# Gated blocks exchanged from SBUF to SBUF, and down's left-side sums begun a group earlier, in a hybrid decoder block on Trainium2

## The chip, the cores and the metric

The kernel runs on one core of one Trainium2 chip. A core has five engines: TensorE (PE; its weight loads are shown apart, as PEld), VectorE (DVE), ScalarE (ACT), GpSimd (POOL) and SyncE (SP). Each has its own queue of instructions and works through it in order; they meet at semaphores. SP, ACT and POOL can issue DMA transfers, and all transfers of the core share 16 DMA engines. SBUF and PSUM are the memories on the chip, each with 128 partitions.

The metric is the device time in microseconds (us) of one execution. The median of three runs before the change is 1948.04 us (1947.73 to 1949.59).

## The reference, cut to what matters

256 rows of 2048 numbers go through one decoder block, all in float32:

```
h = h + 0.5 * swiglu(rms_norm(h, ffn1_norm), ffn1_w_gu, ffn1_w_down)
h = h + hybrid_mixer(rms_norm(h, mix_norm), ...)
h = h + 0.5 * swiglu(rms_norm(h, ffn2_norm), ffn2_w_gu, ffn2_w_down)
gate = sigmoid(rms_norm(h, ple_norm) @ ple_w_gate)
h = h + gate * (p @ ple_w_proj)
out = rms_norm(h, final_norm)

def swiglu(x, w_gu, w_down):
    gate, up = split(x @ w_gu, 2)
    return (silu(gate) * up) @ w_down
```

The change lies in the two swiglu blocks: 2048 inputs, 5632 gate and 5632 up columns, and 2048 outputs each.

## The kernel before, in words

**Products in two halves.** Each float32 operand is split into a high part, rounded to the matmul's type, and a low part, the rest. A product is then three matmuls: high by high, high by low, low by high. For weights a **pair** is a load of 512 KB by SP (line 74, buffers raw, four of them), a cast by ACT (whi, line 77) and a subtraction by DVE (wlo, line 78); it serves 12 matmuls of 128 x 512. `next_weights` (line 85) asks for pairs up to two ahead of their use.

**Groups.** A swiglu block works on 11 column blocks of 512 in three **parts** of 3, 4 and 4 blocks (line 27). For each block a gate/up group ("gu") multiplies the normed input by the gate's block (banks g0, g1 for the two halves of 128 rows) and the up block (u0, u1). When a part's blocks are there, two "dn" groups multiply them by the part's rows of w_down, and add the result to h. At the second swiglu's end one more group ("behind") starts the next gate's product.

**Seven products for eight.** In most groups the first steps of the contraction are done by a seven-product scheme (`SEVEN`, `product`, line 327; tiles shi and slo, lines 298 and 299, are the high and low halves of sums of weights R). It needs sums of the left operand too: `halves` (line 423) makes them on DVE as S, by one addition of the halves (line 455) and four sums (line 461), and splits S into Sh (ACT, line 463) and Sl (DVE, line 464). There is one Sh and one Sl. Four of the seven products read them. The seven products of a group run one by one between the plain pairs of the group in front of it, its *follower* in the code. For down a part with 4 blocks has three steps in the scheme, so its S is made in two pieces; a part with 3 blocks has two, one piece.

**The gated block.** At a gu group's end, silu(gate) comes from ACT (tile sil, line 508) and DVE multiplies it by up (line 480). The block must then be transposed for down: DVE transposes within 32 x 32 tiles (tile tb, line 485), four DMA writes bring quarters of the partitions to DRAM (line 491), and one DMA reads all of it back in the other order (tile tT, line 496). ACT and DVE split it into hTh and hTl (lines 502 and 503), down's left operand.

**What sets the order.** Python generators in `Lanes` (line 720) are advanced one step after each plain pair (`lanes.step`, line 546), and so place side work between pairs. Lane 0 holds the exchange of a gated block, lane 1 the sums. From the traced program a scheduler makes each engine's final order: an instruction that is ready may move ahead, unless `keep_in_program_order` ties it behind its predecessor. Tiles of one tag share their buffers, and a later tile waits until the earlier one's readers are done. In the swiglu's pool the tags sil and tT have one buffer each; S, sil and tb, tT are spread over them.

Of the kernel before, what the change touches and what calls it, by code (L numbers as in the profile page):

```python
# [20 lines left out]
NB = 512  # L21
# [9 lines left out]
NS_DOWN = tuple(3 if i1 - i0 == 4 else 2 for i0, i1 in PARTS)  # L31


SEVEN = (0, 1, 2, 4, 3, 5, 6)
# [12 lines left out]
def block_kernel(ctx, tc, a, out):  # L47
    nc = tc.nc
# [4 lines left out]
    act = ctx.enter_context(tc.tile_pool(name="act", bufs=1))  # L53
# [9 lines left out]
    lanes = Lanes(4)  # L63
    dr = ctx.enter_context(tc.tile_pool(name="dr", bufs=1, space=bass.MemoryType.DRAM))
# [358 lines left out]
    def halves(kind, his, los, ns, wait=0):  # L423


        for _ in range(wait):
            yield
        fp = current[0]

        sh = fp.tile([P, NS, 2, 2, P], F32R, tag="Sh", name="Sh")  # L430
        sl = fp.tile([P, NS, 2, 2, P], F32R, tag="Sl", name="Sl")

        def side(i, g):
            if i in (0, 4, 6):
                k, t = 2 * (g % 2) + (i > 0), i // 6
                c = slice(t * P, (t + 1) * P)
                return his[g // 2][:, k, c], los[g // 2][:, k, c]
            j, t = {1: (1, 1), 2: (0, 0), 3: (0, 1), 5: (1, 0)}[i]
            return sh[:, g, j, t, :], sl[:, g, j, t, :]

        sides[kind] = side

        for g0 in range(0, ns, 2):
            n = min(2, ns - g0)
            hi, lo = his[g0 // 2], los[g0 // 2]
            keep = lambda ins: ins
            if g0 and n == 1:

                keep = tc.keep_in_program_order
                yield  # L450
            if n == 2:
                x = fp.tile([P, 2 * NB], F32, tag="sil", name="S")
            else:
                x = act.tile([P, NB], F32, tag="nat", name="S", bufs=4)
            keep(nc.vector.tensor_tensor(out=x, in0=hi[:, 0:2 * n].bitcast(F32).rearrange("p k x -> p (k x)"),
                                         in1=lo[:, 0:2 * n].bitcast(F32).rearrange("p k x -> p (k x)"), op=ALU.add))
            xv = x.rearrange("p (g j t y) -> p g j t y", g=n, j=2, t=2)
            a11, a12, a21, a22 = (xv[:, :, j, t, :] for t in range(2) for j in range(2))
            for o, y, z, op in ((a22, a21, a22, ALU.subtract), (a21, a11, a21, ALU.subtract),
                                (a11, a22, a11, ALU.subtract), (a12, a11, a12, ALU.add)):  # L460
                nc.vector.tensor_tensor(out=o, in0=y, in1=z, op=op)
            sx = [y[:, g0:g0 + n].rearrange("p g j t y -> p (g j t y)") for y in (sh, sl)]
            nc.scalar.copy(sx[0], x)
            nc.vector.tensor_tensor(out=sx[1], in0=x, in1=sx[0], op=ALU.subtract)
            yield

    def ffn(n, nT, r, scale, next_norm, stat):
        xs = picker(*nT)
        late = callable(r)
        with tc.tile_pool(name="ffn", bufs=1) as fp:  # L470
            hTh, hTl = [], []

            def down_input(u, sil, th, tl, last):

                queue, keep = (nc.sync, lambda x: x) if last else (nc.scalar, tc.keep_in_program_order)
                for t in range(2):
                    nc.vector.scalar_tensor_tensor(out=sil[:, t, :], in0=u[t], scalar=r[:, t:t + 1], in1=sil[:, t, :],  # L480
                                                   op0=ALU.mult, op1=ALU.mult)
                yield
                tb = fp.tile([P, 4, 2, P], F32, tag="tT", name="tb")
                for t in range(2):
                    nc.vector.transpose(tb[:, :, t].rearrange("p c (j x) -> p c j x", j=4),
                                        sil[:, t, :].rearrange("p (j c x) -> p c j x", j=4, c=4))
                if not last:
                    yield
                scr = dr.tile([P, 4, 2, P], F32, tag="scr2", name="scr2", bufs=2)
                for q in range(4):  # L490
                    keep(queue.dma_start(out=scr[:, q].rearrange("(c x) t i -> x c (t i)", c=4),
                                         in_=tb[32 * q:32 * q + 32].rearrange("x c t i -> x c (t i)")))
                for _ in range(2 if last else 4):
                    yield
                tT = fp.tile([P, 4, 2, P], F32, tag="tT", name="tT")
                keep(nc.sync.dma_start(out=tT, in_=scr))
                for _ in range(last or 6):
                    yield
                for t in range(2):
                    hi, lo = (x[:, :, t * P:(t + 1) * P].rearrange("p j (q y) -> p q j y", q=4) for x in (th, tl))  # L500
                    tv = tT[:, :, t].rearrange("p q (j y) -> p q j y", j=4)
                    keep(nc.scalar.copy(hi, tv))  # L502
# [8 lines left out]
            nxt = None  # L511
            current[0] = fp
            lanes.add(1, halves("gu", *nT, NS, 6 if late else 0))
            for group, todo in ffn_plan[n]:
                if group.kind == "behind":
                    break
                dn = group.kind == "dn"
                i0 = PARTS[group.part][0]

                if dn and group.nb and not group.last:  # L520
                    lanes.add(1, halves("gu", *nT, NS))
                elif dn and group.nb and group.follower:
                    lanes.add(1, halves("behind", *nxt, NS_BEHIND, 4))
                elif not dn and group.follower.kind == "dn":
                    lanes.add(1, halves("dn", hTh[i0:], hTl[i0:], NS_DOWN[group.part]))
                if dn and group.last and nxt is None:
                    nxt = new_nT()
                if group.banks is None:
                    group.new_banks()
                for kind, one in todo:  # L530
                    if kind == "seventh":
                        group.follower.product(SEVEN[one])
                        continue
                    b, g = one
                    whi, wlo = next_weights()
                    for j in range(2):
# [3 lines left out]
                        for t in range(2):  # L540
# [3 lines left out]
                            nc.tensor.matmul(out, xh[:, c], wlo[:, j, :], start=False, stop=False, skip_group_check=True)  # L544
                            nc.tensor.matmul(out, xl[:, c], whi[:, j, :], start=False, stop=sp, skip_group_check=True)  # L545
                    lanes.step()
                    if g < len(group.src[b]) - 1:
                        continue
                    outs = group.banks[2 * b:2 * b + 2]
                    if dn:  # L550
                        nb = group.nb + b
                        for t in range(2):
                            hb = h[:, t, block(nb)]
                            nc.vector.scalar_tensor_tensor(out=hb, in0=outs[t], scalar=scale, in1=hb,
                                                           op0=ALU.mult, op1=ALU.add)
                            if group.last:
                                sumsq(stat, t, block(nb), nb)
                        if group.last:
                            norm_block(nxt, next_norm, nb, lambda: fp.tile([P, 2, 4, P], F32, tag="tT", name="tT"),
                                       mm_ps if group.follower or n == "2" else mx_ps)  # L560
                            lanes.advance(0)
                    elif b == 0:
                        if not late:
                            sil = gated(outs)
                    else:
                        if late:
                            r = r()
                            sil = gated(group.banks[0:2])
                            late = False
# [12 lines left out]
                        if last:  # L582
                            lanes.advance(0)
# [797 lines left out]
```

## Time and profile before

| | |
|---|---|
| median of the runs | 1948.04 us |
| the profiled execution | 1948.68 us, span 1947.0 us |
| TensorE busy | 1930.5 us, 99% of the span, 8884 matmuls |
| DVE, ACT, POOL busy | 81%, 60%, 8% |
| mean granted TensorE clock | 0.999 of full speed |
| moved by DMA | 475.04 MB, 244 GB/s |

The profile is of one execution. Its page gives each engine's busy time; views of the trace give groups of instructions by line, the waits (who waited for whom, total us, times, longest), the chain of work that ended last, and timelines with a row for each instruction or run of like ones: start, length, engine, line, operation, out<-in. "SPq" and "ACTq" are these engines' issues of DMAs. Matmuls overlap, so that a row's length is more than the distance to the next start.

### The profile page before, as it was taken

The numbers are of one execution on the slowest core, as the hardware profiler recorded it, in microseconds if no ns is written. First come the engines' busy times: TensorE is split into PE (matmuls) and PEld (weight loads), VectorE is DVE, ScalarE is ACT, GpSimd is POOL, SyncE is SP. The second block draws the span as 40 slices with busy tenths as digits, with TensorE's granted clock in tenths as the row PEclk, the third lists the DMA queues.
The fourth block names the chain that finished last, engine by engine and source line by source line (L and its number), as shares of the span: only waits on it lengthen the run. The fifth ranks groups of instructions, "written<-read, shape, count | busy, mean of one in ns | idle before, by whom it ended". The sixth has DMA issues, their size and how long they took to land.

```text
span 1947.0 us, 24130 instructions
## 1 busy us (share of the span) xinstructions
PE 1930.5 (99%) x8884; PEld 1593.0 (82%) x8884; DVE 1569.3 (81%) x1679; ACT 1163.5 (60%) x1358; POOL 148.4 (8%) x226
## 2 busy tenths in 40 slices
PE   9999999999999999999999999999999999999998
PEld 8888888888888888878788888888888888888886
DVE  7889878997889766797856579899888987888865
ACT  7656666566565557664555456566565755656654
POOL 0011100000010000010100000010000100001000
PEclk9999999999999999999999999999999999999999
DMA  8778888788887765556565786788898987888764
GB/s 314 267 238 282 254 296 273 229 294 250 279 284 240 225 219 170 176 171 208 171 204 160 242 290 227 225 291 283 243 281 249 314 260 240 272 255 293 232 213 144
DMA packets 144182, 475.04 MB, mean 244 GB/s; under 512 B 19649, under 2 KB 47297, under 8 KB 129857
## 3 DMA queue, kind: packets, MB, share of 16 engines
q1 hardware_dynamic: 107200, 302.16, 43.9%
q0 software_dynamic: 25920, 160.44, 30.2%
q10 hardware_dynamic: 10944, 10.91, 1.8%
q8 instruction: 69, 1.13, 0.2%
q14 instruction: 49, 0.39, 0.1%
HBM read 451.44 MB, written 22.02 MB: 243 GB/s over the span
## 4 chain that ended last, share of the span: by engine, by line
PE 88%; DVE 7%; DMA 3%; ACT 1%; issue 1%; POOL 0%; SPq 0%; POOLq 0%; DVEq 0%; ACTq 0%
PE d L545 5%; PE d L543 5%; PE d L544 5%; PE g L343 4%; PE g L344 4%; PE g L342 4%; PE u L544 4%; PE u L545 4%; PE u L543 4%; PE g L544 4%; PE g L545 4%; PE pj L112 4%; PE pj L113 4%; PE pj L114 4%; PE g L543 4%; PE d L343 2%
## 5 line engine op out<-in xcount | busy, mean ns | idle before, releaser
L77 ACT CAST whi<-raw 128x1024 fp32r<-128x1024 f32 (+1 forms) x489 | 512.1, 1050 | 422.7 <-PE pj L114 99.0
L78 DVE TENSOR_TENSOR wlo<-raw,whi 128x1024 fp32r<-128x1024 f32 (+1 forms) x489 | 592.3, 1218 | 162.3 <-ACT whi L77 161.2
L299 DVE TENSOR_TENSOR slo<-R,shi 128x2048 fp32r<-128x2048 f32 (+2 forms) x224 | 444.9, 1989 | 140.0 <-ACT shi L298 138.2
L298 ACT CAST shi<-R 128x2048 fp32r<-128x2048 f32 (+2 forms) x224 | 373.5, 1671 | 128.5 <-DVE R L307 62.7
L112 PE MATMUL pj<-whi,nTh 128*128 128x512 f32 x448 | 179.4, 401 | 0.0
L113 PE MATMUL pj<-wlo,nTh 128*128 128x512 f32 x448 | 175.2, 391 | 1.1 <-DVE wlo L78 1.1
L114 PE MATMUL pj<-whi,nTl 128*128 128x512 f32 x448 | 174.9, 390 | 0.0
L543 PE MATMUL d<-whi,hTh 128*128 128x512 f32 x448 | 174.5, 390 | 0.0
L544 PE MATMUL d<-wlo,hTh 128*128 128x512 f32 x448 | 174.3, 389 | 0.0
L545 PE MATMUL d<-whi,hTl 128*128 128x512 f32 x448 | 173.4, 389 | 0.0
L544 PE MATMUL g<-wlo,nTh 128*128 128x512 f32 x400 | 156.0, 390 | 0.5 <-DVE wlo L78 0.5
L544 PE MATMUL u<-wlo,nTh 128*128 128x512 f32 x400 | 155.7, 389 | 0.4 <-DVE wlo L78 0.4
L545 PE MATMUL g<-whi,nTl 128*128 128x512 f32 x400 | 155.8, 389 | 0.0
L545 PE MATMUL u<-whi,nTl 128*128 128x512 f32 x400 | 155.7, 389 | 0.0
L543 PE MATMUL g<-whi,nTh 128*128 128x512 f32 x400 | 155.3, 390 | 0.0
L543 PE MATMUL u<-whi,nTh 128*128 128x512 f32 x400 | 154.1, 389 | 0.0
L307 DVE TENSOR_TENSOR R<-R 128x2048 f32<-128x2048 f32 (+2 forms) x68 | 135.8, 1996 | 0.1
L113 PEld LDWEIGHTS pj<-wlo,nTh 128*128 128x128 f32 x448 | 84.2, 188 | 18.9 <-DVE wlo L78 2.6
L543 PEld LDWEIGHTS d<-whi,hTh 128*128 128x128 f32 x448 | 84.1, 188 | 18.2 <-ACT hTh L502 1.0
L545 PEld LDWEIGHTS d<-whi,hTl 128*128 128x128 f32 x448 | 84.1, 188 | 17.8
L114 PEld LDWEIGHTS pj<-whi,nTl 128*128 128x128 f32 x448 | 84.1, 188 | 17.5
L544 PEld LDWEIGHTS d<-wlo,hTh 128*128 128x128 f32 x448 | 84.1, 188 | 17.4
(332 smaller groups left out, 3444.1 us busy)
## 6 DMA issues: line engine op xcount, KB each, us to landing
raw<-in_w_gu SPq DMA_DIRECT2D x199, 512.0 KB, 5.7
raw<-in_w_down SPq DMA_DIRECT2D x112, 512.0 KB, 6.9
raw<-in_w_in SPq DMA_DIRECT2D x112, 512.0 KB, 3.4
R<-in_w_gu2q POOLq DMA_DIRECT2D x54, 1024.0 KB, 8.6
R<-in_w_gu1q POOLq DMA_DIRECT2D x48, 1024.0 KB, 8.6
raw<-in_w_out SPq DMA_DIRECT2D x32, 512.0 KB, 4.5
tT<-scr SPq DMA_DIRECT2D x22, 512.0 KB, 5.0
R<-in_w_down11q POOLq DMA_DIRECT2D x12, 768.0 KB, 6.2
```

The source lines that it names most:

```text
L77: nc.scalar.copy(hi[:, j, :], raw[:, j, :])
L78: nc.vector.tensor_tensor(out=lo[:, j, :], in0=raw[:, j, :], in1=hi[:, j, :], op=ALU.subtract)
L112: nc.tensor.matmul(outs[t], xh[:, c], whi[:, j, :], start=st, stop=False)
L113: nc.tensor.matmul(outs[t], xh[:, c], wlo[:, j, :], start=False, stop=False)
L114: nc.tensor.matmul(outs[t], xl[:, c], whi[:, j, :], start=False, stop=sp)
L298: keep(nc.scalar.copy(hi, w))
L299: nc.vector.tensor_tensor(out=lo, in0=w, in1=hi, op=ALU.subtract)
L307: keep(nc.vector.tensor_tensor(out=self.raw[x], in0=self.raw[x], in1=self.raw[y], op=ALU.add))
L343: nc.tensor.matmul(out, xh, wlo[:, g, :], start=False, stop=False, skip_group_check=True)
L543: nc.tensor.matmul(out, xh[:, c], whi[:, j, :], start=st, stop=False, skip_group_check=True)
L544: nc.tensor.matmul(out, xh[:, c], wlo[:, j, :], start=False, stop=False, skip_group_check=True)
L545: nc.tensor.matmul(out, xl[:, c], whi[:, j, :], start=False, stop=sp, skip_group_check=True)
```

## The change

Four things are edited, all in `halves` and `ffn`.

- The exchange: sixteen transfers, all issued by SP, go straight from tb to tT in SBUF, each 32 partitions by 1 KB: quarter q of tb's partitions, column group c, goes to quarter c of tT's partitions, group q. The DRAM scratch, its four writes and the read are gone. ACT issues no transfers here any more.
- Tags: tT takes the buffer of sil, and S takes the buffer of tb (tag tT), for pieces of both lengths. The second piece of S is no longer tied to program order and has no empty step ahead of it.
- Steps: the transfers come four steps after the product with up, the casts two steps later. In a part's last block the transfers come at once and the casts at the step they had. For a group in the seven-product scheme, silu(gate) is taken two pairs after the gate's last pair instead of right behind it.
- Down's sums are traced behind the sixth of the seven products of a part's last gu group (these run in the group in front of it), with their first piece right there; before, they were added at the start of that last group.

```diff
-            keep = lambda ins: ins
-            if g0 and n == 1:
-                keep = tc.keep_in_program_order
-                yield
-            if n == 2:
-                x = fp.tile([P, 2 * NB], F32, tag="sil", name="S")
-            else:
-                x = act.tile([P, NB], F32, tag="nat", name="S", bufs=4)
+            x = fp.tile([P, 2 * NB], F32, tag="tT", name="S")[:, 0:n * NB]
...
-                queue, keep = (nc.sync, lambda x: x) if last else (nc.scalar, tc.keep_in_program_order)
+                keep = (lambda x: x) if last else tc.keep_in_program_order
...
-                if not last:
+                for _ in range(0 if last else 3):
                     yield
-                scr = dr.tile([P, 4, 2, P], F32, tag="scr2", name="scr2", bufs=2)
+                tT = fp.tile([P, 4, 2, P], F32, tag="sil", name="tT")
                 for q in range(4):
-                    keep(queue.dma_start(out=scr[:, q].rearrange("(c x) t i -> x c (t i)", c=4),
-                                         in_=tb[32 * q:32 * q + 32].rearrange("x c t i -> x c (t i)")))
-                for _ in range(2 if last else 4):
-                    yield
-                tT = fp.tile([P, 4, 2, P], F32, tag="tT", name="tT")
-                keep(nc.sync.dma_start(out=tT, in_=scr))
-                for _ in range(last or 6):
+                    for c in range(4):
+                        keep(nc.sync.dma_start(out=tT[32 * c:32 * c + 32, q], in_=tb[32 * q:32 * q + 32, c]))
+                for _ in range(last or 2):
                     yield
...
-                elif not dn and group.follower.kind == "dn":
-                    lanes.add(1, halves("dn", hTh[i0:], hTl[i0:], NS_DOWN[group.part]))
...
                     if kind == "seventh":
-                        group.follower.product(SEVEN[one])
+                        follower = group.follower
+                        follower.product(SEVEN[one])
+                        if not dn and one == 5 and follower.kind == "gu" and follower.follower.kind == "dn":
+                            lanes.finish(1)
+                            lanes.add(1, halves("dn", hTh[i0:], hTl[i0:], NS_DOWN[group.part]))
+                            lanes.advance(1)
                         continue
...
+                    if waiting:
+                        waiting -= 1
+                        if not waiting:
+                            sil = gated(group.banks[0:2])
...
                     elif b == 0:
-                        if not late:
+                        if group.ns:
+                            waiting = 2
+                        elif not late:
                             sil = gated(outs)
...
-                        last = (3 if i1 - i0 == 4 else 2) if len(hTh) == i1 else 0
+                        last = (5 if i1 - i0 == 4 else 4) if len(hTh) == i1 else 0
```

More of the change, by code (lines that the diff above doesn't have):

```diff
@@ L445, in halves @@
             hi, lo = his[g0 // 2], los[g0 // 2]
-            keep = lambda ins: ins
-            if g0 and n == 1:
-                keep = tc.keep_in_program_order
-                yield
-            if n == 2:
-                x = fp.tile([P, 2 * NB], F32, tag="sil", name="S")
-            else:
-                x = act.tile([P, NB], F32, tag="nat", name="S", bufs=4)
-            keep(nc.vector.tensor_tensor(out=x, in0=hi[:, 0:2 * n].bitcast(F32).rearrange("p k x -> p (k x)"),
-                                         in1=lo[:, 0:2 * n].bitcast(F32).rearrange("p k x -> p (k x)"), op=ALU.add))
+            x = fp.tile([P, 2 * NB], F32, tag="tT", name="S")[:, 0:n * NB]
+            nc.vector.tensor_tensor(out=x, in0=hi[:, 0:2 * n].bitcast(F32).rearrange("p k x -> p (k x)"),
+                                    in1=lo[:, 0:2 * n].bitcast(F32).rearrange("p k x -> p (k x)"), op=ALU.add)
             xv = x.rearrange("p (g j t y) -> p g j t y", g=n, j=2, t=2)
@@ L509, in gated @@
                 return sil
-            nxt = None
+            nxt, waiting = None, 0
             current[0] = fp
```

## The prediction, on record before the result

> **What bounds the kernel now.** I read the page's first part, then the waits of TensorE's weight loads, then TensorE's own timeline where these waits lie.
>
> ```profile
> span 1947.0 us, 24130 instructions
> PE 1930.5 (99%) x8884; PEld 1593.0 (82%) x8884; DVE 1569.3 (81%) x1679; ACT 1163.5 (60%) x1358; POOL 148.4 (8%) x226
> PEld d L343 <- DVE slo L299: 4.8, 8, 0.6
> PEld d L543 <- ACT hTh L502: 1.0, 4, 0.3
> ```
>
> TensorE is busy for 99% of the span, and the change takes no matmul away. So only stalls between matmuls can be won. The longest kind within the feed-forward blocks is a down product (tile d, line 343) that waits for the low half of a weight sum (slo), eight times. Two of the eight, in TensorE's timeline, and the last of all, in the chain of waits:
>
> ```profile
> 368.20 0.40 PE L545 MATMUL u<-whi,nTl 128*128 128x512 f32 x1
> 368.73 0.50 PE L343 MATMUL d<-slo,hTh 128*128 128x512 f32 x1
> 369.07 0.40 PE L344 MATMUL d<-shi,hTl 128*128 128x512 f32 x1
> ...
> 376.34 0.39 PE L344 MATMUL d<-shi,Sl 128*128 128x512 f32 x1
> 376.57 0.39 PE L342 MATMUL d<-shi,hTh 128*128 128x512 f32 x1
> 377.18 0.50 PE L343 MATMUL d<-slo,hTh 128*128 128x512 f32 x1 [0.22 <-DVE slo L299]
> 377.52 0.40 PE L344 MATMUL d<-shi,hTl 128*128 128x512 f32 x1
> ```
> ```profile
> 1769.44 0.50 PE d L343
> ```
>
> The first number of a row is its start. A matmul normally starts 0.23 us after the one before (376.34 to 376.57). Here the distances are 0.53 and 0.34, then 0.61 and 0.34: an excess of 0.30 + 0.11 + 0.38 + 0.11 = **0.90 us** for a pair of waits. Eight waits are four pairs, one at the end of part 1 and of part 2 in either feed-forward block: 4 x 0.90 = **3.6 us**. Why slo is late there, by the timeline of DVE with the group of line 461, and by that of ACT:
>
> ```profile
> 345.68 1.22 DVE L455 TENSOR_TENSOR S<-hTh,hTl 128x1024 f32<-128x1024 f32 x1
> L461 DVE TENSOR_TENSOR S<-S 128x256 f32<-128x256 f32 (+1 forms) x92 | 36.7, 399 | 0.9
> 354.09 0.69 DVE L455 TENSOR_TENSOR S<-hTh,hTl 128x512 f32<-128x512 f32 x1
> 363.59 0.68 DVE L464 TENSOR_TENSOR Sl<-S,Sh 128x512 fp32r<-128x512 f32 x1
> 366.92 1.76 DVE L299 TENSOR_TENSOR slo<-R,shi 128x1536 fp32r<-128x1536 f32 x1 [2.65 <-ACT shi L298]
> ```
> ```profile
> 364.92 0.57 ACT L347 COPY d<-d 128x512 f32<-128x512 f32 x1 [1.99 <-PE d L344]
> 365.40 1.48 ACT L298 CAST shi<-R 128x1536 fp32r<-128x1536 f32 x1
> ```
>
> Down's left-side sums S take from 345.68 to 364.27, in two pieces between other work of DVE. Only then can the products that use Sh and Sl end. ACT sits 1.99 us until TensorE is through, copies (364.92), makes the next shi (365.40), DVE makes slo of it (366.92 to 368.68), and TensorE, which has no other matmul left that is ready, starts at 368.73. The late end of S is the cause.
>
> **The change, step by step.** Durations are those of the profiled execution, 1948.68 us (1.7 more than its span). The median of the runs is 1948.04, 0.64 lower; the sum is moved by that at its end.
>
> *1. Down's sums earlier.* They are now written behind the sixth product of the last gate/up group, where the last reader of the old Sh stands, and no longer after the first pair of that group. That is three turns of 12 matmuls ahead (a pair, a product, a pair: 36 x 0.23 = 8 us), and the second piece's empty step and forced order go as well. No operation is added. DVE's share of S is 1.22 + 0.69 + 8 x 0.40, and for the two Sl 1.23 (the first piece's form, as at 1828.53 below) + 0.68: 7.0 us. Is there room in front? Two stretches, the group in front and the last group; the number in the third place behind the length is DVE's busy time:
>
> ```profile
> 297.40:338.00 40.60, 40.60 (x180) 33.62 (x180) 34.66 (x26) 25.01 (x24) 3.96 (x6) 1.00 0.87 265
> 338.00:368.70 30.70, 30.60 (x134) 24.60 (x133) 26.29 (x32) 16.40 (x19) 1.77 (x2) 1.00 0.77 227
> ```
>
> If all of S moved, the front would hold 41.7 of 40.6 us and the last group 19.3 of 30.7. The 1.1 us too much spill over the border, where DVE then has 11 us free. So S ends before the last group's second down product, the products follow their plan, and the four places lose **-3.6 us**. Bounds: 0 (the stall moves) and -4.6 (the waits for hTh, at most 1.0 in all, go too). I take -3.6, since the rows show the cause from end to end.
>
> *2. The exchange.* Removed in each of 22 gated blocks: four writes of 128 KB to DRAM and one load of 512 KB. In 16 blocks ACT issued the writes, in the last block of the six parts SP did. Added: sixteen SP transfers of 32 KB from SBUF to SBUF, with no wait between them and no second trip. The groups of transfers (KB, then us from issue to landing) and SP's timeline at a part's last block:
>
> ```profile
> sc<-dec SPq DMA_DIRECT2D x8, 32.0 KB, 2.4
> raw<-in_w_down SPq DMA_DIRECT2D x112, 512.0 KB, 6.9
> ```
> ```profile
> 381.90 1.78 SPq L491 DMA_DIRECT2D scr<-tb  x4
> 384.71 1.45 SPq L74 DMA_DIRECT2D raw<-in_w_down  x2
> ```
>
> The trace holds no transfer from SBUF to SBUF. Four writes of the same partitions and row length keep SP for 1.78 us, 0.45 each; sixteen take 7.1 us, and by the 32 KB row the last lands 2.4 later: 9.5 us. Today it is 13.1 us from 381.90 to the cast of hTh at 395.03 (next fence). Bounds: 16 x 0.63 + 6.9 = 17 us, were each as slow to issue as the slowest row below and the landing that of a weight load, and 9.5. I take 9.5, from the rows nearest in size and shape. Data that come sooner are worth 0, for hTh ends none of the eight waits; ACT's issue time goes too, and as no matmul waits for that I count nothing.
>
> [...]
>
> *3. What stands behind the sixteen on SP.* SP also loads the split weights, and a load behind the burst is late by up to 7.1 us. In a part's last block, by the timelines of ACT, DVE and PE:
>
> ```profile
> 393.12 1.04 ACT L77 CAST whi<-raw 128x1024 fp32r<-128x1024 f32 x1
> 395.03 1.14 ACT L502 CAST hTh<-tT 128x512 fp32r<-128x512 f32 x2 [0.87 <-DMA tT<-scr]
> 396.55 0.59 ACT L350 COPY part<-d 128x512 f32<-128x512 f32 x1 [0.38 <-PE d L344]
> 397.03 1.48 ACT L298 CAST shi<-R 128x1536 fp32r<-128x1536 f32 x1
> 398.55 1.76 DVE L299 TENSOR_TENSOR slo<-R,shi 128x1536 fp32r<-128x1536 f32 x1
> 402.02 0.39 PE L343 MATMUL d<-slo,Sh 128*128 128x512 f32 x1
> ```
>
> The burst runs from 381.90 to 389.0. The load issued at 384.71 leaves 4.3 us later, lands (6.9) at 395.9, and its cast of 393.12 is 2.8 late. Behind that cast in ACT's queue stand hTh, a copy, shi, and through shi DVE's slo. ACT now idles 0.87 + 0.38 = 1.25 us there, which takes up part of it: slo is 1.55 late. It ends at 400.31 and is used at 402.02, a cover of 1.71, so TensorE waits 0. Without ACT's idle time it would be 1.1 us, at the four last blocks of this kind (parts 1 and 2) 4.4. I take 0. The first block of all is tighter (DVE, PE and the chain of waits):
>
> ```profile
> 54.20 0.70 DVE L485 STREAM_TRANSPOSE tb<-sil 128x512 f32<-128x512 f32 x1
> 64.86 3.49 DVE L78 TENSOR_TENSOR wlo<-raw,whi 128x1024 fp32r<-128x1024 f32 x3
> 71.48 0.39 PE L544 MATMUL g<-wlo,nTh 128*128 128x512 f32 x1
> 57.01 7.52 DMA raw<-in_w_gu
> ```
>
> The load of 57.01 lands at 64.53 and is split at once, as the third of the wlo that end at 68.35, for the matmul at 71.48: cover 3.1. A burst from 54.9 to 62.0 holds it 5.0 us, so TensorE waits **+1.9**, once. Between 0 (the load goes first) and 1.9 I take 1.9, since the transfers are ready 2 us before that load. In the other blocks a pair comes only every second turn and its load has twice that time: 0.
>
> *4. Shared tiles and Silu.* S now shares a buffer with tb, and tT with sil. Silu moves two pairs later and waits for the block before to have left the buffer (hTl, DVE); behind it in ACT's queue stand the casts of weights. hTl is written in the step before, and the product that reads Silu follows two pairs later: 0, up to the cover of 1.71 us if DVE is late by more. At the end of the second feed-forward block, S of the group behind shares its buffer with the norms' tT. S is written one step ahead of the second norm's tT, so it goes first: 0.
>
> Sum: 1948.68 - 3.6 + 1.9 = 1947.0, less 0.64 = **1946.3 us** as the median, 0.09% less. A measurement of this kernel can tell about 0.2% (3.9 us) from no change.
>
> **The other ways.**
>
> *Nothing is added:* the tight load goes ahead of the transfers, and all of step 1's bound is won: 1948.04 - 4.6 = 1943.4, faster. For it: ACT, freed of 64 issues, and the shorter exchange can only help there. Against: it needs every one of these stalls, and the waits for hTh are ended by ACT's order as much as by data.
>
> *The stall moves:* DVE, over-full in front, gives S or the slo of the last gate/up products late, and TensorE waits there instead: 1948.0. Against it: 11 us free in the last group.
>
> *SP holds the weights (slower):* an issue takes more than 0.45 us.
>
> ```profile
> 1821.01 2.54 SPq L186 DMA_DIRECT2D tT<-scr  x4
> ```
>
> Four issues of another pattern take 0.63 each. At that rate the burst is 10.2 us, the load of 384.71 leaves 7.4 late, its cast is 5.9 late, and past idle time and cover 2.9 remain, at four places 11.6. The first block pays 8.1 - 3.1 = 5.0. With step 1's gain: 1948.04 - 3.6 + 16.6 = 1961.0. By the same sum the last blocks begin to pay at a burst of 7.3 us, the gain is used up at 7.6 (0.47 an issue), and the kernel is 0.2% slower at 8.4 (0.52). [...] Against: the row nearest in shape, and the scheduler may put a load between two transfers.
>
> *The group behind waits:* if the second norm had the shared buffer first, S would start after its split, not before.
>
> ```profile
> 1820.62 1.23 DVE L455 TENSOR_TENSOR S<-nTh,nTl 128x1024 f32<-128x1024 f32 x1
> 1828.53 1.23 DVE L464 TENSOR_TENSOR Sl<-S,Sh 128x1024 fp32r<-128x1024 f32 x1 [0.73 <-ACT Sh L463]
> 1833.76 1.67 DVE L162 SCALAR_TENSOR_TENSOR nTl<-tT,gains,nTh 128x256 fp32r<-128x256 f32 x4
> L544 PE MATMUL d<-wlo,hTh 128*128 128x512 f32 x16 | 6.2, 389 | 0.0
> ```
>
> The sums take 9.1 us from 1820.62 to 1829.76. Begun at 1835.4 they end at 1844.6, and the plain matmuls that were left after 1829.9 (16 of each of three kinds, 48 x 0.23 = 11.0 us) last to 1840.9: 3.7 us of wait, 1950.0. Against it: the order of writing.
>
> **Chances.** The forecast 0.42 (own range 1944.2 to 1948.5), nothing added 0.20, the stall moves 0.11, SP holds 0.22, the group behind 0.05. Faster by over 0.2% is below 1944.1: the second case and a little of the first, 0.23. Slower is above 1951.9: the SP case and a little of the last, 0.24. The same: 0.53. The range, 1943.2 to 1955.0, holds the first three cases, the last, and the SP case while its burst is only a little long; about 0.15 is left above and 0.05 below.
>
> **What would show it.** Right: no wait of d L343 for slo at the four places; S ended before the last group's second down product; sixteen issues within some 7 us; hTh's cast within 13 us of the transposes. Wrong: ACT's whi waiting for raw loads by microseconds, or matmuls waiting for wlo or slo right behind the bursts, for then step 3 was too low. If the four stalls stay though S is early, the cause in step 1 is wrong.

## The result

The changed kernel takes **2010.25 us** (median of 4 runs, 2008.99 to 2013.38) against 1948.72 us before (1947.73 to 1949.59): a ratio of 1.0318, 95% interval 1.0300 to 1.0336. It is 3.2% slower. The forecast was 1946.3 us, with a range up to 1955.0; the direction belongs to the rival "SP holds the weights", whose own price was 1961.

### The profile after

First the page of the changed kernel, its own execution of 2008.99 us: span, engines, and the chain that ended last by engine and by line.

```profile
span 2007.3 us, 24510 instructions
PE 1949.3 (97%) x8884; PEld 1600.4 (80%) x8884; DVE 1571.1 (78%) x1679; ACT 1163.5 (58%) x1358; POOL 148.5 (7%) x226
PE 63%; DVE 12%; DMA 10%; SPq 6%; issue 5%; ACT 3%; POOL 0%; DVEq 0%; ACTq 0%; POOLq 0%
```

The work is the same: 8884 matmuls, and DVE and ACT busy within 2 us of before. The span is 60.3 us longer. SP's queue (SPq) now stands in the chain that sets the end, with 6% of the span. TensorE's longest waits, two of ACT's, and these two of ACT's before the change:

```profile
PE d L343 <- DVE slo L299: 16.5, 13, 1.7
PE g L343 <- DVE slo L299: 10.6, 5, 4.1
PE d L342 <- ACT shi L298: 9.5, 6, 2.1
```
```profile
ACT whi L77 <- DMA raw<-in_w_gu: 56.6, 18, 6.5
ACT hTh L490 <- DMA tT<-tb: 40.5, 8, 8.3
```
```profile
ACT hTh L502 <- DMA tT<-scr: 4.5, 4, 1.4
ACT whi L77 <- DMA raw<-in_w_gu: 3.2, 8, 0.7
```

The columns are total us, number of waits and the longest. ACT's rows show two ways in which the transfers cost: weight loads (raw) that leave late, and the exchanged input (tT) that lands late. There is a third: S now shares tb's buffer, so it cannot be written before the transfers have read tb. In five places DVE waited 21.0 us for that. A sixth goes under another name, as one block shows. SP and DVE, by their timelines:

```profile
314.17 14.08 SPq L484 DMA_DIRECT2D tT<-tb  x16
328.35 11.23 SPq L74 DMA_DIRECT2D raw<-in_w_gu  x5
```
```profile
316.23 2.36 DVE L78 TENSOR_TENSOR wlo<-raw,whi 128x1024 fp32r<-128x1024 f32 x2
...
320.70 1.23 DVE L78 TENSOR_TENSOR wlo<-raw,whi 128x1024 fp32r<-128x1024 f32 x1
...
324.90 1.22 DVE L78 TENSOR_TENSOR wlo<-raw,whi 128x1024 fp32r<-128x1024 f32 x1
```

The sixteen issues take SP from 314.17 to 328.25. In that time DVE makes four wlo, and each of them frees one of the four raw buffers, at 317.5, 318.6, 321.9 and 326.1. All four stand empty until SP gets to the loads at 328.35. So the first load is held for 10.9 us, and ACT stands idle for it until 334.61. But TensorE's stop here does not come from that load. ACT, DVE and TensorE, by their timelines:

```profile
326.18 1.91 ACT L298 CAST shi<-R 128x2048 fp32r<-128x2048 f32 x1
334.61 1.04 ACT L77 CAST whi<-raw 128x1024 fp32r<-128x1024 f32 x1 [6.52 <-DMA raw<-in_w_gu]
```
```profile
333.73 1.23 DVE L447 TENSOR_TENSOR S<-hTh,hTl 128x1024 f32<-128x1024 f32 x1 [7.61 <-DMA raw<-in_w_gu]
...
335.81 2.29 DVE L299 TENSOR_TENSOR slo<-R,shi 128x2048 fp32r<-128x2048 f32 x1
```
```profile
338.15 0.56 PE L343 MATMUL g<-slo,Sh 128*128 128x512 f32 x1 [4.10 <-DVE slo L299]
```

TensorE waits for slo. Its input shi was ready at 328.09, but S stood in front of slo in DVE's order, and DVE was idle for 7.61 us before S. The row puts that wait down to a weight load. S reads no weights, though, and the load it names, issued at 328.35, is first used by ACT at 334.61, after S has begun. What S must wait for are the readers of tb: the last of the sixteen transfers, issued at 327.66, took 5.8 us to land, at 333.4, and S starts at 333.73. So this stop comes from the shared buffer behind a long burst. What the held load alone would have cost here, the trace does not tell.

```profile
333.60:338.10 4.50, 0.45 (x2) 0.03 (x1) 4.37 (x5) 3.49 (x4) 0.00 (x0) 1.00 0.78 320
338.10:342.00 3.90, 3.85 (x10) 3.06 (x11) 3.90 (x5) 1.93 (x4) 0.55 (x1) 0.56 0.59 188
```

These are two stretches of the same place: TensorE's busy time and matmuls, then the other engines; the number behind POOL's is the granted clock of TensorE. TensorE stands for 4.3 us, and when it goes on, matmuls start 0.43 us apart and not 0.23 (338.50, 338.93, 339.36 and so on to 341.49), at a granted clock of 0.56: ten matmuls in 3.9 us, where 17 fit.

Over all 22 bursts, by the same reading, the first load behind a burst leaves 7.6 to 14.2 us after its buffer was free, 9.8 on average. A burst is 10.0 to 14.8 us long, 11.9 on average. The row of line 484 says why (ns, least, median, most):

```profile
L484 SPq DMA_DIRECT2D tT<-tb x352: 507/590/2041, 55.3 to 1837.9; - x176
```

With the 0.05 us between two issues, the median pitch is 0.64 us, where the prediction took 0.45. On top of it 59 of the 352 issues took over 0.7 us. In front of each burst SP also stood until tb was made, 78.9 us in 22 waits.

Where TensorE's time went can be counted. Outside the mixer, take the excess: what the distance between the starts of neighbouring matmuls has beyond 0.227 us. Excesses over 0.3 us, the stops, hold 6.1 us before and 53.1 after; those between 0.1 and 0.3 hold 3.0 and 16.6. The two differences, 47.0 + 13.6 = 60.6 us, are the longer span. Of the small ones, 55 after and none before are the step of 0.40 to 0.46 us of the slow clock; they hold 11.0 us, so nearly a fifth of the loss is the slow clock behind the stops and not the stops.

Each stop can also be followed back, from the matmul to what it waited for and on along the engines, until a transfer ends the wait (with S put down to the transfers that it waits for, as above). Of the 53.1 us, about 16 go back to hTh waiting for tT, about 14 to S waiting for tb's readers, and about 19 to casts of weights waiting for their loads; under 5 us end elsewhere. So the late input, by its two ways, stopped TensorE for longer than the held loads did.

The slow clock came behind some stops and not behind others. Behind the stop above (4.3 us) the granted clock was 0.50 from 338.46 to 341.87, for 3.4 us, with the matmuls 0.43 us apart. It was 0.50 for 3.4 us as well behind two stops of 1.9 and 2.0 us that lie 2.3 us apart (407.99 and 410.24) and behind a single one of 2.7 us (596.81). It was not behind single stops of 1.6 us (389.23 and 1564.34), nor behind one of 3.0 us (1513.76). No run shows what decides it.

### The profile page after: what moved, and what is told of

It reads as the page before. It is cut to its first block, busy times and chain, and to the rows that moved or that the text cites. A ratio compares the mean times of both kernels' runs of the same rounds, so it can differ in the third digit from the quotient of the medians.

```text
span 2007.3 us, 24510 instructions
## 1 busy us (share of the span) xinstructions
PE 1949.3 (97%) x8884; PEld 1600.4 (80%) x8884; DVE 1571.1 (78%) x1679; ACT 1163.5 (58%) x1358; POOL 148.5 (7%) x226
## 4 chain that ended last, share of the span: by engine, by line
PE 63%; DVE 12%; DMA 10%; SPq 6%; issue 5%; ACT 3%; POOL 0%; DVEq 0%; ACTq 0%; POOLq 0%
SPq L484 6%; DMA raw<-in_w_gu 5%; PE pj L112 4%; PE pj L113 4%; PE pj L114 4%; PE d L535 3%; PE d L536 3%; PE d L534 3%; DVE slo L299 3%; DVE wlo L78 3%; PE g L343 3%; PE g L344 3%; PE g L342 3%; PE g L535 3%; PE g L536 3%
## 5 line engine op out<-in xcount | busy, mean ns | idle before, releaser
L299 DVE TENSOR_TENSOR slo<-R,shi 128x2048 fp32r<-128x2048 f32 (+2 forms) x224 | 444.8, 1986 | 99.6 <-ACT shi L298 98.1
L114 PEld LDWEIGHTS pj<-whi,nTl 128*128 128x128 f32 x448 | 84.1, 188 | 17.6
```

What stands on the lines that cost most here:

```text
L114: nc.tensor.matmul(outs[t], xl[:, c], whi[:, j, :], start=False, stop=sp)
L299: nc.vector.tensor_tensor(out=lo, in0=w, in1=hi, op=ALU.subtract)
```

## The experiments

Theory Q: the burst holds SP's queue, and weight loads stand behind it. Against it theory L: the exchanged input lands too late, or waits on shared buffers. Theory T: the traffic of the small packets. Theory S: the earlier sums do it. All times are medians, against the kernel before on the same chip. For two kernels "lost by" a point is the difference of the start times of the n-th matmul, of 8884 in either.

### The exchange without the earlier sums, and the sums without the exchange

```diff
 (e1: changed kernel)
-                        if not dn and one == 5 and follower.kind == "gu" and follower.follower.kind == "dn":
-                            lanes.finish(1)
-                            lanes.add(1, halves("dn", hTh[i0:], hTl[i0:], NS_DOWN[group.part]))
-                            lanes.advance(1)
+                elif not dn and group.follower.kind == "dn":
+                    lanes.add(1, halves("dn", hTh[i0:], hTl[i0:], NS_DOWN[group.part]))
```

> The changed kernel with down's left-side sums put back to where they stood before (behind the first pair of a part's last group); the sixteen transfers, the buffers and the later silu stay. Theory Q (the burst holds SP's queue, and weight loads stand behind it): the loss stays, 2005 to 2020 us, and the bursts are as long as in the changed kernel (10 to 15 us each). Theory S (the earlier sums make the loss, because they share a buffer with the transposed block and wait for its transfers): most of the loss goes, under 1970 us.

Measured: **2027.5 us**, ratio 1.0408 (1.0392 to 1.0424). This is above theory Q's range. The exchange is the loss, and the earlier sums took 17 us off it. They had to: S now shares a buffer with the transposed block tb, and so does not start before the transfers have read the tb in front of it. What ended DVE's idle time before S, in this run:

```profile
DMA tT<-tb: 31.3, 7
```

Theory S falls as it was put: the earlier sums are not the loss, they escape part of it. The shared buffer is another matter: followed back as above, about 33 us of this run's 65 us of stops end at S waiting for the transfers.

```diff
 (e2: kernel before; parts 1 and 2)
-        for g0 in range(0, ns, 2):
-            n = min(2, ns - g0)
+        one = kind == "dn"
+        for g0 in range(0, ns, 1 if one else 2):
+            n = 1 if one else 2
...
+            if one:
+                x = act.tile([P, NB], F32, tag="nat", name="S", bufs=4)
...
+                        if group.part and not dn and one == 5 and follower.kind == "gu" and follower.follower.kind == "dn":
+                            lanes.finish(1)
+                            lanes.add(1, halves("dn", hTh[i0:], hTl[i0:], NS_DOWN[group.part]))
+                            lanes.advance(1)
```

> The kernel before with only down's sums earlier, in parts 1 and 2: the first two quarters behind the sixth product of the group in front, one quarter at a time in a buffer of the activations' pool (so no buffer is shared with a transfer); the third quarter in the first step of the last group, since its input comes through DRAM only then. Step 1 of the prediction taken alone: the four waits of 0.9 us at the ends of parts 1 and 2 shrink or go, 1944 to 1948 us against 1948.7. If the stall only moves, or DVE is over-full in front, 1948 to 1950.

Measured: **1953.78 us**, ratio 1.0024 (1.0015 to 1.0033), a little slower, and above both ranges. TensorE's waits of d L343 for slo shrink only from 4.8 us (8 times) to 3.7 (5 times), and in front of each of the four places, 9 to 14 us ahead, there is a new stop of 1.4 us, one of them here:

```profile
353.26 0.61 PE L548 MATMUL u<-whi,nTh 128*128 128x512 f32 x2
355.11 0.50 PE L549 MATMUL u<-wlo,nTh 128*128 128x512 f32 x1 [1.23 <-DVE wlo L78]
```
```profile
334.00:356.00 22.00, 20.77 (x92) 16.90 (x91) 20.88 (x33) 8.92 (x11) 1.43 (x2) 1.00 0.62 171
```

DVE is busy for 20.88 of those 22 us, and wlo is late. That is the rival "the stall moves", in this form of the edit: it sums a quarter at a time, in more and shorter instructions, and the third quarter has to wait for an input that still comes at the old step. So it does not yet judge the earlier sums as the change makes them; the last run does.

### Transfers that nobody waits for

```diff
 (e3: kernel before)
+                idle = act.tile([P, NB], F32, tag="junk", name="idle", bufs=1)
+                for q in range(4):
+                    for c in range(4):
+                        keep(nc.sync.dma_start(out=idle[32 * c:32 * c + 32, 128 * q:128 * q + 128],
+                                               in_=tb[32 * q:32 * q + 32, c, 0]))
```

> The kernel before, with sixteen more transfers of SP in each gated block, from the transposed block into a scratch buffer that nobody reads (512 bytes a row, half the bytes of the real ones), just ahead of the load of the transposed block. Theory Q: nobody waits for them, and it loses all the same, as SP issues 16 x 0.64 us ahead of the weight loads: 1985 to 2015 us. Theory L (the loss is that the exchanged block itself lands late, or that it shares buffers): 1948 to 1955 us.

Measured: **2075.69 us**, ratio 1.0652 (1.0635 to 1.0668). Sixteen more issues in a block cost here even where no data depend on them. But the run lost more than expected, and not cleanly: the kernel's own load of tT stands behind the sixteen, so its input is late as well, and SP also waited for the scratch buffer:

```profile
SPq L501 <- DMA idle<-tb: 28.1, 19, 4.9
```
```profile
PE d L548 <- ACT hTh L507: 40.1, 6, 10.7
```

So it does not rule theory L out.

### Four at a time

```diff
 (e4: changed kernel)
-                for _ in range(0 if last else 3):
-                    yield
                 tT = fp.tile([P, 4, 2, P], F32, tag="sil", name="tT")
                 for q in range(4):
                     for c in range(4):
                         keep(nc.sync.dma_start(out=tT[32 * c:32 * c + 32, q], in_=tb[32 * q:32 * q + 32, c]))
-                for _ in range(last or 2):
+                    yield
+                for _ in range(last - 4 if last else 1):
                     yield
```

> The changed kernel with the sixteen transfers handed out four at a time over four steps of the lanes, so that one or two weight loads stand between; the input is cast in the same step as before. Theory Q: a hold of 4 x 0.64 = 2.6 us is inside the loads' cover, most of the loss goes: 1950 to 1975 us. Theory L or a theory of traffic (the small packets slow the weight transfers): as many transfers and bytes, and the last of them later, so no better than 2010 us.

Measured: **2014.76 us**, ratio 1.0338 (1.0323 to 1.0352): no better, which is theory L's or T's number and not Q's. But the edit did not do what it says, as SP's timeline shows:

```profile
313.17 0.33 SPq L74 DMA_DIRECT2D raw<-in_w_gu  x1
316.59 14.27 SPq L482 DMA_DIRECT2D tT<-tb  x16
330.95 11.32 SPq L74 DMA_DIRECT2D raw<-in_w_gu  x5
```

Only the first block's were apart. In the other 21 the sixteen still go out side by side, though weight loads are written between the fours: the order on the queue is the scheduler's, and it had put them together. The run tells nothing on length; a later one does it by data.

### Another queue

```diff
 (e5: changed kernel; e6: the same for q of 2 and 3 alone; e7: e5 with e1's edit)
-                        keep(nc.sync.dma_start(out=tT[32 * c:32 * c + 32, q], in_=tb[32 * q:32 * q + 32, c]))
+                        keep(nc.gpsimd.dma_start(out=tT[32 * c:32 * c + 32, q], in_=tb[32 * q:32 * q + 32, c]))
```

> The changed kernel with all sixteen transfers issued by POOL and not by SP; same bytes, same rows, same buffers, same waits. Theory Q (what costs is SP's queue held ahead of the weight loads): the hold falls on POOL's queue of quarter loads R, which are asked for long ahead, so the loss goes but for a few us: 1944 to 1965 us. Theory T (the traffic of small packets, or the waits on shared buffers, costs): 2000 to 2015 us, as before.

> The changed kernel with eight of the sixteen transfers on SP and eight on POOL. Theory Q: a burst of 8 x 0.64 = 5.1 us and more with waits, half the hold, and the loss falls by more than half, since the loads have some cover: 1950 to 1980 us. Theory T: as many small packets as before, 2000 to 2015 us.

Measured: **1992.69 us** with all on POOL, ratio 1.0225 (1.0209 to 1.0241), and **2004.91 us** with half on either, 1.0288 (1.0273 to 1.0304). All on POOL lies between the ranges of Q and T and fits neither. Half on either lies in the range of T, but the run on POOL with slack, below, speaks against T. With all on POOL the held loads are gone, and something else has taken their place:

```profile
ACT hTh L490 <- DMA tT<-tb: 77.3, 19, 6.0
...
ACT whi L77 <- DMA raw<-in_w_gu: 3.4, 7, 1.0
```

Weight loads cost 3.4 us of ACT's time, as before the change. But ACT now stands at the cast of the input for 77.3 us, and the casts of weights and the shi stand behind it in its queue. From the end of the transposes to the last landing it is 12.6 us before the change (mean of 22 blocks), 15.5 in the changed kernel, and 18.2 here; the cast was moved from 22.7 us behind the transposes to 17.6. So theories Q and L each have a part: with the held loads gone, 18 us are won and 44 stay.

> The transfers on POOL as in the run above, and down's left-side sums where they stood before the change. If the earlier sums are worth 17 us by themselves (2027.5 against 2010.3 with the burst on SP), it is about 17 us slower than the run above; if they only gave cover against the held queue, the two are within 4 us of each other: 1946 to 1965 us.

With e1's edit on top, the sums at their old place: **2068.99 us**, ratio 1.0616 (1.0600 to 1.0632), 76 us slower than e5, where 17 or next to nothing was expected. The shared buffer is the cause: S waits for slower transfers to have read tb, and TensorE for S's high half.

```profile
PE d L342 <- ACT Sh L455: 78.3, 6, 14.8
```

### The change without its transfers

```diff
 (e8: changed kernel)
+                scr = dr.tile([P, 4, 2, P], F32, tag="scr2", name="scr2", bufs=2)
+                for q in range(4):
+                    keep(queue.dma_start(out=scr[:, q].rearrange("(c x) t i -> x c (t i)", c=4),
+                                         in_=tb[32 * q:32 * q + 32].rearrange("x c t i -> x c (t i)")))
...
                 tT = fp.tile([P, 4, 2, P], F32, tag="sil", name="tT")
-                for q in range(4):
-                    for c in range(4):
-                        keep(nc.sync.dma_start(out=tT[32 * c:32 * c + 32, q], in_=tb[32 * q:32 * q + 32, c]))
+                keep(nc.sync.dma_start(out=tT, in_=scr))
```

> The changed kernel with the way through DRAM put back (four writes by ACT, or by SP in a part's last block, and one load by SP, at the step in which the transfers stand), and all else of the change kept: the swapped buffers, the later silu, the earlier sums. Theory Q: no burst, so no more than the input's lateness, 1948 to 1965 us. If the swapped buffers or the later silu cost by themselves, it is over 1980 us.

Measured: **1947.34 us**, ratio 0.9992 (0.9982 to 1.0001): not to be told from before. Swapped buffers, later Silu and earlier sums cost nothing that shows. All of the 63 us between this run and the changed kernel come with the sixteen transfers, be it through the queue or through the data and buffers that wait for them.

### Hold and lateness apart

```diff
 (e9: kernel before, SP; e10: the same with nc.gpsimd)
-                scr = dr.tile([P, 4, 2, P], F32, tag="scr2", name="scr2", bufs=2)
...
-                tT = fp.tile([P, 4, 2, P], F32, tag="tT", name="tT")
-                keep(nc.sync.dma_start(out=tT, in_=scr))
+                tT = [act.tile([P, 2, 2, P], F32, tag="nat", name="tT", bufs=4) for _ in range(2)]
+                for q in range(4):
+                    for c in range(4):
+                        keep(nc.sync.dma_start(out=tT[q // 2][32 * c:32 * c + 32, q % 2], in_=tb[32 * q:32 * q + 32, c]))
```

> The kernel before (its sums, its silu, its steps, its cast of the input 22 to 30 us behind the transposes) with the sixteen direct transfers on SP in place of the way through DRAM, into two buffers of the activations' pool, so that nothing new is shared. The input has the old slack, so what is left is the hold of SP's queue alone. Theory Q (the hold is the main loss): 1985 to 2025 us. If the loss is rather that the input lands too late for the earlier casts: 1948 to 1960 us.

> The same with the transfers on POOL: neither SP held nor the casts early. In the run on POOL without slack ACT stood at the input's cast 19 times, 77 us in all, for transfers that landed 18 us behind the transposes on average. If that was its loss (44 us), it goes: 1948 to 1960 us. If POOL's held quarter loads or the traffic of small packets cost: 1970 to 1995 us.

Measured: **2023.89 us** on SP, ratio 1.0382 (1.0355 to 1.0409), and **1960.1 us** on POOL, 1.0058 (1.0045 to 1.0072). The two differ in the issuing queue alone. ACT's waits, first on SP, then on POOL:

```profile
ACT whi L77 <- DMA raw<-in_w_gu: 98.1, 22, 9.7
ACT hTh L502 <- DMA tT<-tb: 25.7, 7, 5.3
```
```profile
ACT hTh L502 <- DMA tT<-tb: 15.2, 10, 2.9
...
ACT whi L77 <- DMA raw<-in_w_gu: 5.3, 8, 2.0
```

This is the plainest pair of the study. Issuing from SP and not from POOL costs 64 us, with the same transfers, bytes and buffers: loads are held, and the input lands 14.5 us behind the transposes on SP against 12.2 on POOL (means of 22 blocks). S does not wait in either run. Theory T falls, for the small packets run on POOL too. What is left on POOL, 11 us, is lost mostly at the last blocks of parts 1 and 2 (stops of 2.4, 2.2, 2.0 and 2.9 us), where the cast has no slack. The 33 us between e5 and e10 go with the input's slack, but sums and buffers differ there too.

### Spread by the data

```diff
 (e11: the run e9; all but the last blocks of the parts)
-                for t in range(2):
-                    nc.vector.transpose(tb[:, :, t].rearrange("p c (j x) -> p c j x", j=4),
-                                        sil[:, t, :].rearrange("p (j c x) -> p c j x", j=4, c=4))
...
+                for c in range(4):
+                    for t in range(2):
+                        keep(nc.vector.transpose(tb[:, c, t].rearrange("p (j x) -> p j x", j=4),
+                                                 sil[:, t, :].rearrange("p (j c x) -> p c j x", j=4, c=4)[:, c]))
+                    for q in range(4):
+                        keep(nc.sync.dma_start(out=tT[q // 2][32 * c:32 * c + 32, q % 2], in_=tb[32 * q:32 * q + 32, c]))
+                    if not last:
+                        yield
```

> The run on SP with slack, with the transposes of all but a part's last blocks cut into four by columns, one in each of four steps, and the four transfers that read each behind it: here the data keep the four groups apart, where the scheduler had put the sixteen of the run spread over four steps side by side. A hold is at most 4 x 0.64 = 2.6 us. Theory Q: the sixteen blocks inside the parts lose nothing, the six last blocks of the parts as before: 1955 to 1980 us, clearly under the run on SP with slack. If it is the number of issues and not the length of the hold: no better than that run.

Measured: **2001.29 us**, ratio 1.0260 (1.0240 to 1.0280): 23 us better than e9, 20 short of what was expected. This time loads do stand between the transfers, though not between all four groups: in every block eight or more still go out side by side, as here on SP's timeline:

```profile
318.86 5.78 SPq L490 DMA_DIRECT2D tT<-tb  x8
324.74 1.19 SPq L74 DMA_DIRECT2D raw<-in_w_gu  x1
326.03 3.50 SPq L490 DMA_DIRECT2D tT<-tb  x4
329.63 0.53 SPq L74 DMA_DIRECT2D raw<-in_w_gu  x1
330.26 4.29 SPq L490 DMA_DIRECT2D tT<-tb  x4
```

ACT's wait for gate/up loads falls from 98.1 to 5.2 us with as many issues, so the length of the hold is what matters there. For down's loads it rises from 5.9 to 15.6 us. The rest is lost at the last blocks, which kept their full bursts (6.9 us at that of part 1 in the first feed-forward block, 7.1 at that of part 2 in the second), and around the third block of a part (3.9 us in part 1, against 8.3 in e9). There Sh comes late, by the timelines of SP and ACT:

```profile
359.64 4.39 SPq L490 DMA_DIRECT2D tT<-tb  x7
364.12 0.54 SPq L74 DMA_DIRECT2D raw<-in_w_down  x1
```
```profile
372.18 1.04 ACT L77 CAST whi<-raw 128x1024 fp32r<-128x1024 f32 x1 [3.85 <-PE u L547]
373.13 1.04 ACT L463 CAST Sh<-S 128x1024 fp32r<-128x1024 f32 x1
```

The last sum of S ended at 370.49, but Sh stands in ACT's queue behind a cast of weights, which begins at 372.18. TensorE had just freed the buffer that it writes, and its load, issued at 364.12 behind eight transfers side by side (seven of them lie in the view), had just landed, at 372.1. At the other three places like this ACT's wait for that cast, 3.5 to 4.0 us, ends with the load. So part of the hold is still there; how much of the rest it makes up was not tried.

### The way through DRAM, with one load later

```diff
 (e12: the run e8)
-                for _ in range(2):
+                for _ in range(2 + slow):
                     yield
                 tT = fp.tile([P, 4, 2, P], F32, tag="sil", name="tT")
...
-                        gen = down_input(outs, sil, th, tl, last)
+                        gen = down_input(outs, sil, th, tl, last, 2 if group.follower.kind == "gu" and not group.follower.ns else 0)
```

> The changed kernel with the way through DRAM put back (1947.3 us), and in the first block alone the load of the transposed block two steps later. In that kernel SP stood at this load from 55.0 to 65.2 us, with weight loads behind it, and TensorE lost 2.2 us between 66 and 80 us. If that wait is the cause, it goes: 1944.5 to 1946.5 us, 0.1 to 0.2% under the kernel before.

Measured: **1945.05 us** (11 runs, 1943.26 to 1949.37) against 1948.96, ratio **0.9985** (0.9976 to 0.9994). This is faster than both kernels, by a little. Between 60 and 80 us it loses 0.2 us where e8 lost 2.2, as expected. TensorE's weight loads, their longest groups of waits in the whole run:

```profile
PEld g L539 <- DVE wlo L78: 2.9, 4, 1.0
PEld pj L113 <- DVE wlo L78: 2.6, 4, 0.9
PEld vp L1113 <- issue: 1.6, 1, 1.6
```

The eight waits of d L343 for slo, 4.8 us before, are no longer among them. At the four ends of parts 1 and 2 TensorE gains 1.2, 1.2, 1.1 and 1.2 us on the kernel before, 4.7 in all. Some 1.6 us are lost before 60 us, at the start; that was not looked into.

## Why the prediction was wrong

**Step 1, the earlier sums, was right where nothing else delays S.** It took -3.6 us between 0 and -4.6. In e12 the four places give -4.7, a little past the far bound, and the waits named are the ones that go. Where the sums are cut smaller and the input comes late, e2, the rival "the stall moves" comes true at the same places.

**Step 2 was mis-sized, and fatally.** It took 0.45 us for an issue from the row nearest in shape, a write from SBUF to DRAM. The transfers between two places of SBUF took SP 0.59 each (median) and 0.05 to the next, with stretches up to 2.04: a burst of 11.9 us on average, not 7.1. The input landed 15.5 us behind the transposes, where 9.5 was taken and the way through DRAM needs 12.6. So the exchange was not even the shorter way, and "data that come sooner are worth 0" had the sign wrong: they came later, to a cast that had been moved 5 us earlier, and about 16 us of TensorE's stops go back to hTh waiting for tT. The slower end of its bounds, 0.63 and 17 us, was about the truth; choosing the other end was the mistake.

**Step 3 failed in its "0 in the other blocks".** It rested on a pair of weights that comes only every second turn and a load that has twice that time. The four raw buffers come free within some 9 us, and a burst of 12 holds all of them at once, so that the loads leave in a row. About 19 us of stops go back to weight loads, most of them behind bursts; by the count of matmuls 4.3 us are lost behind the third block of part 2 (613 to 628 us, times of before), a block that was put at nothing.

**Step 4 put the shared buffers at 0, and that failed too.** It asked who else holds the buffers of Silu and of the second norm, and not when the sixteen transfers would have read the tb that S shares. Alone the swap costs nothing (e8). Together with slow transfers S waited six times for them, 28.6 us in all with the wait shown above, and about 14 us of stops go back to it: 6.0 us by the count of matmuls around 314 to 345 us, behind the second block of part 1, and 4.5 around 560 to 590, behind the second of part 2. With the sums at their old place it is 76 us (e7 against e5).

So one size, the burst's, was wrong, and three terms that were put at nothing hung on it: the input's lateness, the loads of the inner blocks, and S.

**The rival "SP holds the weights" had the queue and its deciding point** (0.47 us an issue; 0.64 came). Its price of 16.6 us for held loads is near the 19 us of stops that go back to them, but that is luck: it had five blocks with one load late in each, and the stops came mostly behind third blocks. It lacked the late input, S, and the slow clock behind some of the stops (11.0 us). With a chance of 0.22 it was also too unlikely: its "against" was a row of another kind of transfer.

That the transfers are small is not what cost in the runs: e10 moves the same sixteen in a block and loses 11 us in all. What counted was the time on the issuing queue, 64 us between e9 and e10, and what waited for the data.

## What to carry to other kernels

Count what stands behind a burst on its queue, and for how long: compare the burst's length with the time in which the buffers behind it come free, in every block and not only in the tightest. Ask of each buffer that the transfers read or write who needs it next. When a row names what ended a wait, ask whether the waiting instruction reads or overwrites that at all. Where the trace has no row of the same kind of transfer, take the slow end of the bounds for the issue, and move the transfers to a queue that has nothing urgent behind it (64 us between e9 and e10), or let the data space them (23 us between e9 and e11), since the written order alone may not (e4). And count what comes behind a stop of TensorE too: here 11.0 of the 60.6 us lay in slow matmuls behind the stops.

## What was not expected of the hardware

- A transfer of 32 rows of 1 KB from SBUF to SBUF took SP 0.59 us to issue, and a weight load of 512 KB 0.33 us (medians of the changed kernel, lines 484 and 74). On POOL such a transfer took 0.50, and 0.72 at most (e10).
- On SP 59 of the 352 issues took 0.7 to 2.04 us, 58 of them while weight loads (raw or R) were under way; but so were 218 of the other 293. What they wait for is not shown by a run.
- Between 338 and 1827 us of the changed kernel the granted clock was 0.50 six times, for 3.4 us (four times) or 6.8 us (twice), each time behind a stop of 2.7 or 4.3 us or behind two stops of 1.6 to 2.3 us close together. Other such stops had none behind them (3.0 us at 1513.76; 1.7 and 1.6 us at 645.58 and 647.38). Slow matmuls hold 11.0 us of the 60.6 lost.
